# A head that sums on TensorE, later sums ahead of a mixer, and a routing with priority, in a two-block transformer kernel on one core

## The chip, the cores and the metric

The kernel runs on one core of one Trainium2 chip. The metric is the device time of an execution in microseconds; less is better. The profile times every instruction of one execution. TensorE (PE, with its weight loads as PEld), VectorE (DVE), ScalarE (ACT) and GpSimd (POOL) compute, SyncE (SP) issues most transfers. [...]

## The reference, cut to what matters

512 tokens of width 1024 pass through two blocks in float32. The first has two attention branches and a mixture of 16 experts with two experts per token, the second a mixer and an MLP twice. The parts that the change touches are these:

```python
# first_block: the head
c_act = silu(c)
mod = c_act @ ada_w + ada_b          # six vectors: shift1, scale1, gate1, shift2, scale2, gate2
h = rmsnorm(x, norm1_g) * (1 + scale1) + shift1
proj = h @ w_in
...
# hierarchical_moe: a softmax over 4 groups, the best group, its best two of 4 experts
y = hierarchical_moe(rmsnorm(x, norm2_g) * (1 + scale2) + shift2, ...)
...
# second_block, end of layer 0 and start of layer 1
x = x + rms_norm(sq_relu_mlp(h, w1, w2), norm_mlp_post[0])
h = rms_norm(x, norm_mix_pre[1])
m = mixer_c(h, ...)
```

## The kernel before, in words

Activations stand transposed, features on the 128 partitions in 8 chunks (k) and tokens along the free axis. A float32 product is made of three products of rounded parts: every operand is split into a high part (a cast on ScalarE) and a low part (a subtraction on VectorE), and `mm3` (L196, L199, L200) issues high by high, high by low and low by high. Weights come as slabs of 128 x 1024 through a ring of raw buffers, loaded by SP (L188, L1130) and split by `split` (L168 on ScalarE, L169 on VectorE).

**The head** is `first_products`. It lies under a manual schedule: on each of the five engines the instructions run in the order of the code. x comes in four transfers, then the first quarter of the modulation's weights (`fetch(0)`, L609), then slabs. ScalarE squares x chunk by chunk (L644, L647), VectorE adds the squares up (L648), four products with a column of ones sum over the partitions (`col_sum`, L326), GpSimd takes the power -0.5 (L344), and four products spread the result over the partitions (L353). The first modulation is made in quarters q of 256 shift and 256 scale columns: `ada` multiplies eight raw chunks by their entry of c and adds them on VectorE (L617, L619, L620), `columns` sums over the partitions with four single-column products (L628) and turns the sums into factors on ScalarE (L631, L632), and `modulate` makes two chunks of h (L636 and L638 on ScalarE, L639 on VectorE). x was multiplied by the norm before (L654, seven of eight chunks on GpSimd). The products of five slabs (two queries, two keys, and the forget gate as number 2) accumulate in five banks; quarter q of h gives each slab two chunks, six products. `NAT` is the slab behind which the next quarter's `columns` and `modulate` stand, `NPE` how many of the eight terms go to TensorE as raw chunks. A float32 product with one column shows as two records.

**The routing.** `route_half` makes the logits of half the tokens (L1072, two transposes L1075, the copy L1076) and the rows of the normed tokens (additions L1082 on GpSimd and VectorE, transposes L1085, copies L1086). `route` is some hundred small VectorE instructions (from L1372); in it `early` makes the one-hot rows (L1220) and gathers the first expert's tokens by products with the token rows (L1225). Two weight slabs are split ahead of the expert loop, held behind the last instruction `last_hi` of the norm on ScalarE. Outside the manual schedule a scheduler orders every engine by priority, which is the order of the code unless `first(n)` raises it by n places. After the routing a branch on the number of overflowing tokens stands on all engines, then the experts' loop.

**The sums for the second mixer.** `halves` makes the last product of an MLP in two halves of the tokens; `post` does the norm and the residual of a half chunk by chunk, as a side line that advances one step with each step of the main line (`weave`). At the end of it the squares' sums for the next norm go to TensorE (`col_mean`, four products L326), `mix_left` takes the power on GpSimd (L1552) and spreads it (L1557). `LATE[save][hb]` is the number of steps that half hb lets pass before these sums; `LATE[1]` is for the first MLP, ahead of `mixer_c`, where the second half's side line advances half a step per step of the main line.

## Time and profile before

| | us |
|---|---|
| median of 3 runs | 2283.05 |
| lowest and highest run | 2279.7 and 2284.46 |
| the profiled execution, its own time | 2282.78 |
| its span from the first to the last instruction | 2281.1 |
| TensorE busy | 2167.1 (95%) |
| VectorE busy | 1393.0 (61%) |
| ScalarE busy | 1109.9 (49%) |
| GpSimd busy | 422.6 (19%) |

The page gives busy times, the span in 40 slices with the granted clock, and the costliest groups. A timeline row has start, length, engine, line, operation, tiles written <- read, shapes and count; in brackets stand the idle time of the engine before it and what ended that. A window row gives busy time and count of each engine in a stretch, and the granted clock.

### The profile page before, as it was taken

How to read it: one execution, taken by the hardware profiler on the slowest of the kernel's cores; microseconds unless marked ns; L12 is line 12 of the kernel's file. 1: busy time of each engine (PE TensorE's matmuls, PEld its weight loads, DVE VectorE, ACT ScalarE, POOL GpSimd, SP SyncE). 2: the span in 40 equal slices, each digit the busy share in tenths (PEclk: the TensorE clock that was granted, in tenths of full speed). 3: DMA queues.
4: the chain of work that ended last, by engine and by line, in shares of the span. 5: the costliest groups of instructions: out<-in, count | busy, mean ns of one | idle time of the engine just before them, and what ended most of it. 6: DMA issues, size and time to landing. Idle time of an engine off the chain costs nothing. (4 is left out here: it accounts for less than half of the span.)

```text
span 2281.1 us, 31923 instructions
## 1 busy us (share of the span) xinstructions
PE 2167.1 (95%) x12164; PEld 1809.7 (79%) x12164; DVE 1393.0 (61%) x2002; ACT 1109.9 (49%) x1856; POOL 422.6 (19%) x468
## 2 busy tenths in 40 slices
PE   5999999979999999899999999999999999999996
PEld 4778778967888788678998888997666689888886
DVE  8577775568999964666543344565767846344343
ACT  3545542348888854445553233443655647332231
POOL 4111000231111142110400000350324433000004
PEclk9999999989999989999999999999999999999998
DMA  6464265569999741224332222342122142332321
GB/s 242 140 185 118 88 204 164 184 223 345 353 358 355 270 154 45 69 78 151 100 111 97 98 94 100 110 135 55 49 71 54 43 158 89 117 101 93 101 74 38
DMA packets 127154, 320.08 MB, mean 140 GB/s; under 512 B 24751, under 2 KB 30127, under 8 KB 126994
## 3 DMA queue, kind: packets, MB, share of 16 engines
q1 hardware_dynamic: 111934, 286.56, 36.8%
q0 software_dynamic: 11200, 22.91, 4.2%
q10 hardware_dynamic: 3860, 8.51, 1.0%
q8 instruction: 97, 1.59, 0.3%
q14 instruction: 63, 0.52, 0.1%
HBM read 296.31 MB, written 18.69 MB: 138 GB/s over the span
## 5 line engine op out<-in xcount | busy, mean ns | idle before, releaser
L196 PE MATMUL acc<-h_hi,w_hi 128*128 128x512 f32 (+1 forms) x1464 | 515.7, 352 | 3.5 <-DVE q L429 1.5
L200 PE MATMUL acc<-h_hi,w_lo 128*128 128x512 f32 (+1 forms) x1464 | 509.1, 348 | 1.2 <-DVE w_lo L169 1.2
L199 PE MATMUL acc<-h_lo,w_hi 128*128 128x512 f32 (+1 forms) x1464 | 508.7, 348 | 0.0
L169 DVE TENSOR_TENSOR w_lo<-x_raw,w_hi 128x1024 fp32r<-128x1024 f32 x260 | 317.8, 1231 | 189.8 <-ACT w_hi L168 185.2
L168 ACT CAST w_hi<-x_raw 128x1024 fp32r<-128x1024 f32 x260 | 271.0, 1046 | 283.8 <-PE acc L199 246.6
L196 PEld LDWEIGHTS acc<-h_hi,w_hi 128*128 128x128 f32 x1464 | 279.5, 191 | 36.9 <-issue 2.7
L200 PEld LDWEIGHTS acc<-h_hi,w_lo 128*128 128x128 f32 x1464 | 278.9, 190 | 35.9 <-DVE w_lo L169 2.5
L199 PEld LDWEIGHTS acc<-h_lo,w_hi 128*128 128x128 f32 x1464 | 279.0, 191 | 29.7 <-issue 0.7
L169 DVE TENSOR_TENSOR w_lo<-w_raw,w_hi 128x1024 fp32r<-128x1024 f32 (+2 forms) x141 | 166.8, 1184 | 145.0 <-ACT w_hi L168 141.3
L168 ACT CAST w_hi<-w_raw 128x1024 fp32r<-128x1024 f32 (+2 forms) x141 | 143.6, 1019 | 222.1 <-PE acc L199 199.3
L196 PE MATMUL acc<-act_hi,w_hi 128*128 128x512 f32 (+1 forms) x640 | 223.0, 349 | 0.0
L199 PE MATMUL acc<-act_lo,w_hi 128*128 128x512 f32 (+1 forms) x640 | 222.6, 348 | 0.0
L200 PE MATMUL acc<-act_hi,w_lo 128*128 128x512 f32 (+1 forms) x640 | 222.4, 348 | 0.0
L283 POOL TENSOR_TENSOR acc<-acc,sq 128x256 f32<-128x256 f32 x60 | 55.5, 926 | 721.0 <-ACT sq L282 720.2
L196 PEld LDWEIGHTS acc<-act_hi,w_hi 128*128 128x128 f32 x640 | 121.9, 190 | 15.3 <-ACT act_hi L1621 0.3
L199 PEld LDWEIGHTS acc<-act_lo,w_hi 128*128 128x128 f32 x640 | 121.9, 190 | 15.0
L200 PEld LDWEIGHTS acc<-act_hi,w_lo 128*128 128x128 f32 x640 | 121.8, 190 | 15.0
L506 DVE TENSOR_TENSOR pl<-pexp,ph 128x512 fp32r<-128x512 f32 x144 | 113.9, 803 | 25.9 <-ACT ph L505 25.1
L1626 DVE TENSOR_TENSOR m<-m,acc 128x512 f32<-128x512 f32 (+1 forms) x64 | 35.2, 552 | 138.7 <-PE acc L200 138.7
L470 DVE TENSOR_REDUCE mx<-acc 128x1 f32<-128x128 f32 x192 | 89.2, 484 | 37.9 <-PE acc L469 36.3
L504 ACT ACTIVATE pexp<-sT 128x512 f32<-128x512 f32 x144 | 82.5, 573 | 32.2 <-PE sT L495 14.2
L196 PE MATMUL gu<-w_hi,xh 128*128 128x512 f32 x240 | 95.5, 398 | 0.0
(593 smaller groups left out, 4422.0 us busy)
## 6 DMA issues: line engine op xcount, KB each, us to landing
x_raw<-mlp_w SPq DMA_DIRECT2D x90, 512.0 KB
w_raw<-mlp_w SPq DMA_DIRECT2D x48, 512.0 KB
x_raw<-w_down SPq DMA_DIRECT2D x40, 512.0 KB
x_raw<-w_up SPq DMA_DIRECT2D x39, 512.0 KB
x_raw<-w_gate SPq DMA_DIRECT2D x38, 512.0 KB
w_raw<-w_in SPq DMA_DIRECT2D x20, 512.0 KB
h_raw<-w_up SPq DMA_DIRECT2D x19, 512.0 KB
h_raw<-w_gate SPq DMA_DIRECT2D x18, 512.0 KB
```

Source lines behind the costliest of these rows:

```text
L168: nc.scalar.copy(hi[:, :n], raw[:, :n])
L169: (eng or nc.vector).tensor_sub(lo[:, :n], raw[:, :n], hi[:, :n])
L196: mm(ps, l[0], r[0], start=start, stop=False)
L199: mm(ps, l[0], r[1], start=False, stop=False)
L200: return mm(ps, l[1], r[0], start=False, stop=stop).ins
L283: (eng or nc.gpsimd).tensor_add(acc[:, a:a + 256], acc[:, a:a + 256], sq)
L470: self.last_max = nc.vector.reduce_max(mx[:, c0 + qb:c0 + qb + 1], ps[:, :n], axis=AX.X).ins
L504: nc.scalar.activation(e[:, :o], ps[:, :o], AF.Exp)
L506: nc.vector.tensor_sub(pt[1][:, :o], e[:, :o], pt[0][:, :o])
L1626: nc.vector.tensor_add(self.m[:, i, tok], self.m[:, i, tok], ps)
```

## The change

In the head the squares are no longer added on VectorE: each chunk's square goes to TensorE as four products with a column of ones. The first quarter's eight raw chunks go to TensorE as well, four ahead of the spread of the norm and four behind it; of the later quarters three of eight (`NPE = 3`). The multiplication by the norm joins that by the scale on VectorE (`scale`), and the head's first slabs are split behind the first modulation. The third and fourth slab are loaded ahead of the second quarter. `NAT` becomes one value per quarter. `LATE[1]` goes from (34, 10) to (44, 14). In the routing the logits' two VectorE instructions and all of `route` get a priority 4000 places higher, and the two slabs split ahead wait for the last one-hot row on VectorE instead of the norm on ScalarE.

```diff
@@ -50,8 +50,8 @@
 RATE = 1.0
 APB = 2
 EV = 1000
-NPE = 0
-NAT = 1
+NPE = 3
+NAT = (3, 2, 2)
 GY = 2
 VK = 1
 PK = 1
@@ -59,7 +59,7 @@
 R1 = 0.4
 R5 = 0.4
 APP = 0
-LATE = ((40, 22), (34, 10))
+LATE = ((40, 22), (44, 14))
 
 
 
@@ -610,7 +610,7 @@
                 return [out[k // 2][:, k % 2 * 512:k % 2 * 512 + 512] for k in range(NC)]
 
             def ada(raws):
-                acc = [sp.tile([P, 512], F32, name="ada_sum", bufs=4) for i in range(2)]
+                acc = [sp.tile([P, S], F32, name="ada_sum", bufs=4) for i in range(2)]
                 for k in range(NC - NPE):
                     ck, a = self.c_act[:, k:k + 1], acc[k % 2]
                     if k < 2:
@@ -620,39 +620,49 @@
                 nc.vector.tensor_add(acc[0], acc[0], acc[1])
                 return acc[:1]
 
-            def columns(q, raws, acc):
-                src = [(raws[k], self.c_act[:, k:k + 1]) for k in range(NC - NPE, NC)]
-                for l, r in src + [(a, self.ones[:, :1]) for a in acc]:
+            def columns(q, raws, ks, acc=()):
+                for l, r in [(raws[k], self.c_act[:, k:k + 1]) for k in ks] + [(a, self.ones[:, :1]) for a in acc]:
                     for c in range(4):
                         d = 8 * (c // 2) + 2 * q + c % 2
                         nc.tensor.matmul(pa[:, d:d + 1], l[:, c * P:(c + 1) * P], r, start=False, stop=True,
                                          skip_group_check=True)
+
+            def mods(q):
                 for k in (2 * q, 2 * q + 1):
                     nc.scalar.mul(self.mod[:, 8 + k:9 + k], pa[:, 8 + k:9 + k], self.v("norm1_g", k))
                 nc.scalar.copy(self.mod[:, 2 * q:2 * q + 2], pa[:, 2 * q:2 * q + 2])
 
-            def modulate(q):
-                for k in (2 * q, 2 * q + 1):
-                    nc.scalar.mul(x[:, k], x[:, k], self.mod[:, 8 + k:9 + k])
-                    b = self.mod[:, k:k + 1]
-                    nc.scalar.activation(self.h[0][:, k], x[:, k], AF.Identity, bias=b)
-                    nc.vector.scalar_tensor_tensor(self.h[1][:, k], x[:, k], b, self.h[0][:, k], op0=OP.add,
-                                                   op1=OP.subtract)
+            def scale(k):
+                nc.vector.scalar_tensor_tensor(x[:, k], x[:, k], self.mod[:, 8 + k:9 + k], r, op0=OP.mult, op1=OP.mult)
+
+            def parts(k):
+                b = self.mod[:, k:k + 1]
+                nc.scalar.activation(self.h[0][:, k], x[:, k], AF.Identity, bias=b)
+                nc.vector.scalar_tensor_tensor(self.h[1][:, k], x[:, k], b, self.h[0][:, k], op0=OP.add,
+                                               op1=OP.subtract)
 
             raws = [fetch(0)]
-            acc = sp.tile([P, S], F32, name="acc", tag="ada_sum", bufs=4)
-            nc.scalar.square(acc, x[:, 0])
-            for k in range(1, NC):
+            cs = self.pn.tile([P, S], F32, name="csum", tag=self.ntags[0])[:, :4]
+            nc.tensor.matmul(cs, self.zb, self.zb[:, :4], start=True, stop=True)
+            for k in range(NC):
                 sq = sp.tile([P, S], F32, name="sq", bufs=2)
                 nc.scalar.square(sq, x[:, k])
-                nc.vector.tensor_add(acc, acc, sq)
+                for j in range(4):
+                    nc.tensor.matmul(cs[:, j:j + 1], sq[:, j * P:(j + 1) * P], self.ones[:, :1], start=False, stop=True,
+                                     skip_group_check=True)
             c = sp.tile([P, 4], F32, name="rs_c")
-            nc.scalar.activation(c, self.col_sum([acc]), AF.Identity, bias=self.eps, scale=1.0 / D)
-            r = self.spread(self.rsqrt(c), sp)
-            sums = [ada(raws[0])]
-            for k in range(NC):
-                (nc.gpsimd if k else nc.vector).tensor_mul(x[:, k], x[:, k], r)
-            slabs = [self.slab(w[i], NC) for i in range(2)]
+            nc.scalar.activation(c, cs, AF.Identity, bias=self.eps, scale=1.0 / D)
+            c = self.rsqrt(c)
+            columns(0, raws[0], range(4))
+            r = self.spread(c, sp)
+            columns(0, raws[0], range(4, NC))
+            mods(0)
+            scale(0)
+            scale(1)
+            parts(0)
+            slabs = [self.slab(w[0], NC)]
+            parts(1)
+            slabs.append(self.slab(w[1], NC))
             raw = sp.tile([P, NC * 16], F32, name="fa_raw")
             nc.sync.dma_start(raw, self.t["w_fa"])
             fa = tuple(sp.tile([P, NC, 16], F32R, name=n) for n in ("fa_h", "fa_l"))
@@ -660,11 +670,9 @@
             nc.scalar.copy(fa[0], rv)
             nc.vector.tensor_sub(fa[1], rv, fa[0])
             slabs.append(fa)
+            slabs += [self.slab(w[i], NC) for i in (2, 3)]
             raws.append(fetch(1))
-            columns(0, raws[0], sums[0])
-            modulate(0)
-            sums.append(ada(raws[1]))
-            slabs += [self.slab(w[i], NC) for i in (2, 3)]
+            sums = ada(raws[1])
             ps = [pp.tile([P, S], F32, name="pst") for _ in range(3)] + [self.ptile() for _ in range(2)]
 
             def mm(n, q):
@@ -673,16 +681,19 @@
                     self.mm3(ps[n][:hi.shape[-1]], (hi[:, k], lo[:, k]), (self.h[0][:, k], self.h[1][:, k]), k == 0,
                              k == NC - 1)
 
-            for q in range(4):
+            for q in range(3):
                 if q < 2:
                     raws.append(fetch(q + 2))
-                    sums.append(ada(raws[q + 2]))
                 for n in range(5):
-                    if q < 3:
-                        mm(n, q)
-                        if n == NAT:
-                            columns(q + 1, raws[q + 1], sums[q + 1])
-                            modulate(q + 1)
+                    mm(n, q)
+                    if n == NAT[q]:
+                        columns(q + 1, raws[q + 1], range(NC - NPE, NC), sums)
+                        mods(q + 1)
+                        for k in (2 * q + 2, 2 * q + 3):
+                            scale(k)
+                            parts(k)
+                        if q < 2:
+                            sums = ada(raws[q + 2])
             mm(2, 3)
             fg = self.forget(ps[2], tmp, sp.tile([16, S], F32R, name="nf_h", tag="sq", bufs=2), nf)
             next(fg)
@@ -1069,11 +1080,13 @@
             self.mm3(ps[:20, :256], (self.rw[0][:, k], self.rw[1][:, k]), (h[0][:, k], h[1][:, k]),
                      k == 0, k == NC - 1)
         lt = self.rp.tile([P, 256], F32, name="rf", bufs=2)
-        nc.vector.tensor_scalar(lt[:20], ps[:20, :256], self.rb, None, op0=OP.add)
+        with self.first(4000):
+            nc.vector.tensor_scalar(lt[:20], ps[:20, :256], self.rb, None, op0=OP.add)
         ps = self.ptile()
         for b in range(2):
             nc.tensor.transpose(ps[:, 20 * b:20 * b + 20], lt[:20, b * P:(b + 1) * P], self.idf[:20, :20])
-        nc.vector.tensor_copy(self.L[:, 2 * hb:2 * hb + 2], ps[:, :40].rearrange("p (b c) -> p b c", b=2))
+        with self.first(4000):
+            nc.vector.tensor_copy(self.L[:, 2 * hb:2 * hb + 2], ps[:, :40].rearrange("p (b c) -> p b c", b=2))
         yield 1
         for k in range(0, NC, 2):
             ps = self.ptile()
@@ -1217,8 +1230,8 @@
                 nc.vector.tensor_add(m, E[:, 0, :, 0], E[:, 1, :, 0])
                 oh = mp.tile([P, NC, P], F32R, name="oh", tag="xl").bitcast(F32)
                 for b in range(4):
-                    nc.vector.tensor_scalar(oh[:, b], self.slot, pos[:, b, 0:1], m[:, b:b + 1], op0=OP.is_equal,
-                                            op1=OP.mult)
+                    self.last_oh = nc.vector.tensor_scalar(oh[:, b], self.slot, pos[:, b, 0:1], m[:, b:b + 1],
+                                                           op0=OP.is_equal, op1=OP.mult).ins
                 ps = [self.ptile().rearrange("p (k t) -> p k t", k=4) for _ in range(2)]
                 for k in range(NC):
                     for b in range(4):
@@ -1226,7 +1239,8 @@
                                          start=(b == 0), stop=(b == 3))
                 return ps
 
-            idx, sw, nov, ovx, ftok, ps = self.route(rp, mp, pt, early)
+            with self.first(4000):
+                idx, sw, nov, ovx, ftok, ps = self.route(rp, mp, pt, early)
             for q in range(2):
                 c = slice(4 * q, 4 * q + 4)
                 nc.scalar.copy(x[0][:, c], ps[q])
@@ -1235,7 +1249,7 @@
             my = self.pool(es, "moe_y")
             gather(1, xgs[1])
             self.parts = deque(self.pairs(self.wp, 2) + self.pairs(xw, 1))
-            with tc.issue_after(self.last_hi):
+            with tc.issue_after(self.last_oh):
                 split = [parts(*ahead.popleft()) for _ in range(2)]
             hl, self.parts = self.parts, deque(self.pairs(xw, 1))
             n = nc.values_load(nov[0:1, 0:1], min_val=0, max_val=7)
```

## Rows read from the trace of the kernel before

**Rows 1.** The page, parts 1 and 5.
```profile
PE 2167.1 (95%) x12164; PEld 1809.7 (79%) x12164; DVE 1393.0 (61%) x2002; ACT 1109.9 (49%) x1856; POOL 422.6 (19%) x468
...
L168 ACT CAST w_hi<-x_raw 128x1024 fp32r<-128x1024 f32 x260 | 271.0, 1046 | 283.8 <-PE acc L199 246.6
```

**Rows 2.** Windows: PE, PEld, DVE, ACT, POOL busy (count); clock; DMA.
```profile
38.00:43.00 5.00, 5.00 (x16) 3.35 (x17) 5.00 (x8) 3.07 (x7) 0.00 (x0) 0.50 0.93 317
826.00:834.80 8.80, 8.73 (x41) 8.73 (x42) 5.01 (x11) 5.09 (x15) 3.17 (x5) 0.50 0.29 95
1477.20:1483.60 6.40, 6.01 (x26) 5.74 (x27) 2.04 (x5) 1.94 (x6) 4.65 (x5) 0.50 0.91 297
1511.20:1517.90 6.70, 6.70 (x33) 6.62 (x33) 4.59 (x9) 2.45 (x7) 3.97 (x10) 0.50 0.90 269
```

**Rows 3.** Timeline of the head: start, length, engine, line, tiles, count.
```profile
5.80 0.63 ACT L644 ACTIVATE acc<-x 128x512 f32<-128x512 f32 x1 [2.77 <-DMA x<-x]
...
19.76 1.81 PE L628 MATMUL acc<-ones,ada_sum 128*128 128x1 f32 x8
...
20.67 12.26 POOL L654 TENSOR_TENSOR x<-x,rstd 128x512 f32<-128x512 f32 x7 [2.83 <-ACT rstd L356]
21.57 4.17 DVE L169 TENSOR_TENSOR w_lo<-x_raw,w_hi 128x1024 fp32r<-128x1024 f32 x2 [0.26 <-ACT w_hi L168]
...
28.74 0.79 PE L199 MATMUL pst<-h_lo,w_hi 128*128 128x512 f32 x1 [3.47 <-DVE h_lo L639]
...
33.35 0.40 PE L200 MATMUL pst<-h_hi,w_lo 128*128 128x512 f32 x1
```

**Rows 4.** Timeline of the head's last rounds, 48.8 to 70 us.
```profile
49.05 0.95 PE L628 MATMUL acc<-ones,ada_sum 128*128 128x1 f32 x8
...
49.86 0.40 PE L196 MATMUL pst<-h_hi,fa_h 128*16 128x512 f32 x1
...
58.92 0.72 ACT L638 ACTIVATE h_hi<-x,mod 128x512 fp32r<-128x512 f32 x1
...
59.68 0.75 DVE L639 SCALAR_TENSOR_TENSOR h_lo<-x,mod,h_hi 128x512 fp32r<-128x512 f32 x1 [5.64 <-ACT h_hi L638]
...
65.79 1.23 DVE L169 TENSOR_TENSOR w_lo<-w_raw,w_hi 128x1024 fp32r<-128x1024 f32 x1 [1.64 <-ACT w_hi L168]
...
68.50 0.39 PE L200 MATMUL acc<-h_hi,w_lo 128*128 128x512 f32 x1
```

**Rows 5.** Timeline of the routing, 485 to 510 us.
```profile
485.68 2.34 DVE L169 TENSOR_TENSOR w_lo<-w_raw,w_hi 128x1024 fp32r<-128x1024 f32 x2
...
485.81 0.30 PE L1075 MATMUL acc<-idf,rf 20*128 20x20 f32 x2 [0.42 <-DVE rf L1072]
...
486.24 2.45 POOL L1082 TENSOR_TENSOR rf<-h_half 128x256 f32<-128x256 f32 x1 [5.19 <-PE acc L1075]
...
487.95 0.18 DVE L1076 COPY L<-acc 128x40 f32<-128x40 f32 x1
488.06 0.91 DVE L1082 TENSOR_TENSOR rf<-h_half 128x256 f32<-128x256 f32 x1
...
493.67 0.58 ACT L1086 COPY rows<-acc 128x512 f32<-128x512 f32 x1 [0.85 <-PE acc L1085]
...
496.29 9.49 PE L1225 MATMUL acc<-oh,rows 128*128 128x128 f32 x64 [0.59 <-DVE oh L1220]
...
509.87 0.47 PE L196 MATMUL gu<-w_hi,x_raw 128*128 128x512 f32 x1 [3.60 <-PEq L1244]
```

**Rows 6.** Timeline of TensorE, 1474 to 1510 us.
```profile
1477.23 0.56 PE L326 MATMUL csum<-ones,acc 128*128 128x1 f32 x2 [3.08 <-DVE acc L283]
...
1481.99 1.23 PE L1557 MATMUL spread<-idf,mix_rcol 128*128 128x128 f32 x4 [0.36 <-POOL mix_rcol L1552]
...
1509.38 0.35 PE L326 MATMUL csum<-ones,acc 128*128 128x1 f32 x2 [2.07 <-DVE acc L283]
```

**Rows 7.** Timeline of TensorE, 818 to 840 us.
```profile
826.07 2.72 PE L1320 MATMUL gu<-gg,sq 128*128 128x2 f32 x12 [0.84 <-ACT sq L1318]
```

## The prediction

> **What bounds the kernel now.** I read the page's busy times first: TensorE is busy for 95% of the span [rows 1]. [...] Then the table of windows, for the granted clock of single stretches [rows 2]; the timeline of the head [rows 3, 4]; the timeline of the routing [rows 5]; and TensorE's timeline where the second block's first MLP hands over to the second mixer [rows 6], with one row of the same engine for the clock [rows 7]. In all of them the reader should look at what the next product of TensorE waits for.
>
> In the head the 120 products of the first five slabs are held up until 28.74 us, because the low parts are late (VectorE's two splits took 4.17 us beside seven multiplications on GpSimd, 12.26 us); 12 are done by 33.75 and all by 68.9 [rows 3, 4]. From 49.86 to 68.50 there are 78 products and one group of four single-column products of 0.81 us (49.05 to 49.86): (18.87 - 0.81) / 78 = 0.23 us a product [rows 4]. The window of 38 to 43 us was at half clock [rows 2], and a single-column product (two records) took 1.81 us for four early in the head, so 0.43 us each without the tail, against 0.20 us at full clock [rows 3, 4].
>
> **Part 1, the head.** It moves three sums from VectorE to TensorE as products with one column. Removed: the adding up of the squares and the eight-term sums of the first modulation on VectorE, three of eight terms in the three later ones, the multiplication of x by the norm on GpSimd and one ScalarE pass per chunk. Added: 32 - 4 products for the squares, 32 - 4 for the first modulation's columns, 12 more for each of three later ones. The order in this block is the order in the code on every engine, so it can be walked.
>
> The first square ends at 6.43 [rows 3]. 32 products at 0.43 are 13.8 us, the 32 of the first modulation as much again, and the spread of the norm between them, four products too, some 1.8: 35.8 us. A square takes ScalarE 0.63 us [rows 3] against 1.7 for its four products, so TensorE sets the pace. Only then do the modulation's factors go out: 0.3, the scaling on VectorE 0.75 (the same form and size as the low part), the high part on ScalarE 0.72 [rows 4], then the first slab's cast of 1.05 [rows 1], which now stands behind them: first product at 38.7. On VectorE follow a split (1.23), a low part (0.75) and a split (1.23) [rows 4]: the second slab's products are free at 41.9, and 12 are done at about 44, which was 33.75 before. What else the diff touches in this block (names, the loop's bounds) issues nothing. That is 10.3 us later; the cost of GpSimd beside VectorE is gone and is counted in it.
>
> The other 108 products: 108 x 0.23 = 24.8 us; three groups of 16 single-column products at 0.20 = 9.7 us. After each group the next round needs factors, scaling, high and low part twice in turn: 0.3 + 2 x (0.75 + 0.72 + 0.75) and some handing over, 5.0 us, and 0.46 us of products behind it. The first time only one slab (1.38) and the round's own first slab (1.38) lie beside that, a wait of 2.7; the two other times two slabs do, a wait of 1.3 each: 5.3 us. Before, three slabs stood there, and rounds two and three did not wait. Half clock behind the start and behind the longest waits: 3 us (between 0 and 6). The sum is 44 + 42.8 = 86.8 against 68.9: **+17.5 us** (+15 to +21). Loads: the slabs' weights go ahead of the second modulation's on SP, whose buffers are free at 27 and 36 us, far ahead of their use; the third and fourth come free with the splits. If that cover is gone, a load of 512 KB costs some 1.7 us at the 317 GB/s of 38 to 43 us [rows 2]. TensorE has no other work that could hide the head, so I count it in full.
>
> Everything hangs on the clock in the two runs of single-column products. The nearest rows: from 826.07 TensorE runs two-column products back to back (12 records in 2.72 us), and from 826 to 834.8 it is busy for 8.73 of 8.80 us, with wider products towards the end; the clock reads 0.50 throughout [rows 2, 7]. So I take the lower level. [...]
>
> **Part 2, the routing.** Now the copy of the logits waits for two splits of prefetched weights on VectorE (485.68, 2.34 us) and ends up at 487.95, and a token row's addition of 0.91 follows before the first routing step [rows 5]. Its transposes end at 486.1 [rows 5]. Ahead of both it wins 1.75 + 0.9 us, and something from GpSimd, whose token row took 2.45 us beside the splits. The token rows, due before the products at 496.29, were in place at 494.25 [rows 5]; they start earlier too, as the splits are gone. I take **-3 us**, down to -4.5. The MoE's first product at 509.87 follows from this chain [rows 5]. The splits come behind the one-hot rows and have until the first product for it; the reload of their two buffers on SP comes later by as much, for products that are some slabs away. In the other direction: the splits were tied to a ScalarE instruction and are now tied to a VectorE one, so the two casts of 1 us may go ahead of the norm's activations there, and up to +2 us is possible.
>
> **Part 3, the later sums.** TensorE waits 3.08 us for the squares at 1477.23, 0.36 at 1481.99, 2.07 at 1509.38 [rows 6], and both times half clock follows: 6.01 us busy at 0.50, then 6.70 [rows 2]; half of each is lost. Together 5.5 + 3.0 + 3.35 = 11.9 us. Ten steps later in the first half puts 30 products of half the width ahead of the sums, some 3.5 us; four steps later in the second half are eight steps of the main work with six such products each, some 5.5 us. Both are more than the wait. What is late next: the spread, which needs the power on GpSimd. From the end of the sums (1477.23 + 1.7) it took until 1481.99, 3 us [rows 6], and now two steps, 0.7 us, stand between. New waits of 2.4 us in all, so **-9.5 us** (-5 to -11.9). The second half's weights are split by then and VectorE has pauses, so nothing else need be late.
>
> **The sum.** +17.5 - 3 - 9.5 = +5 us. The profiled execution took 2282.78 us (span 2281.1), 0.3 under the median of 2283.05. I say 2288 us. Some 0.2%, 4.6 us, is about what a measurement of this kernel can tell from no change, so the forecast lies at that bound.
>
> **The rivals.**
> - *The single-column products raise the clock.* Place: the sums of squares. After some ten products at 0.43 the other 54 take 0.20 each: the factors go out at about 23 us; with some 9 to the twelfth product and 39.8 for the rest, plus 1 to 2 of half clock, the products end at about 73.4, +4.5. With the other parts -8 us: 2275. For it: the engine is busy without a pause for 29 us. Against: 826 to 834.8 [rows 2, 7]. A rise at time t saves half of what is left up to 35.8, so it decides the sign from a rise before about 26 us on. Chance 0.18.
> - *The sums for the mixer only wait elsewhere.* The spread is held for the full 3 us both times, and the clock falls as before. Then part 3 gives 4, and the sum is +10.5: 2293. For it: the power stands behind additions on GpSimd. Against: those have time while TensorE goes on. Chance 0.12.
> - *The routing does not move.* VectorE's order is made by the scheduler, and the copy may still land behind other work, or the casts go in front. Part 2 is 0 to +2, and the sum +8 to +10: 2292. Chance 0.08.
>
> **How the numbers follow.** The forecast has 0.62; its own range is 2282 to 2294 from the bounds of the parts. About half of it lies over the bound of 4.6 us and half within. The first rival is nearly all faster, the others slower. Faster 0.19, same 0.35, slower 0.46. The range reaches from the middle of the first rival to above the second: 2275 to 2297.
>
> **What would show it.** In the changed profile: the first product of the slabs near 39 us and the last near 87; single-column products 0.43 us apart up to 36 us; no wait over 1 us before the two sums at the mixer and a clock of 1.00 behind them; the logits' copy directly behind its transpose, and the MoE's first product 20.8 us after the end of that transpose instead of 23.8. The head's last product below 75 us, or a new wait before the mixer's spread, would make the prediction wrong.

## The result, and the profile after

| | before | after |
|---|---|---|
| median (6 runs each) | 2283.64 us | 2308.95 us |
| lowest and highest | 2279.7 and 2285.77 | 2302.15 and 2316.11 |
| ratio, 95% interval | | 1.011 [1.0091, 1.0128] |
| span of the profiled execution | 2281.1 us | 2306.2 us |

The change makes the kernel slower by 1.1%. The forecast was 2288 us with a range to 2297: the direction was right, the size lies outside.

The page of the kernel after, its head and part 1, where [rows 1] stand for before:

```profile
span 2306.2 us, 32250 instructions
PE 2206.1 (96%) x12349; PEld 1847.3 (80%) x12349; DVE 1375.7 (60%) x1984; ACT 1105.9 (48%) x1848; POOL 409.2 (18%) x461
```

VectorE, ScalarE and GpSimd lost a little work, and TensorE, which bounds the kernel, got 39 us more. Where in time the 25.1 us came can be read by following the same instruction through both timelines:

| instruction | before | after | later by |
|---|---|---|---|
| the head's last product of 512 columns | 68.50 | 88.56 | 20.06 |
| the transposes of the logits | 485.81 | 508.05 | 22.24 |
| the experts' first product | 509.87 | 532.45 | 22.58 |
| the norm's spread (L353) ahead of the second mixer | 1459.18 | 1480.08 | 20.90 |
| the first product of scores (L468) behind that mixer | 1580.07 | 1604.03 | 23.96 |
| the end | 2281.1 | 2306.2 | 25.1 |

So in this pair of profiles the head costs 20 us, the routing's stage neither gives nor takes, and the mixer's stage, which should have given 9.5 us, takes 3.1. The other shifts, of 1.1 to 2.2 us and not all of one sign, lie in stages that the change does not touch.

**The head.** TensorE's timeline after, against [rows 3, 4] (start, length, engine, line, tiles, count; in brackets the idle time before and what ended it):

```profile
6.33 13.81 PE L651 MATMUL csum<-ones,sq 128*128 128x1 f32 x64 [2.37 <-ACT sq L649]
20.00 6.96 PE L627 MATMUL acc<-c_act,w_raw 128*128 128x1 f32 x32
26.83 2.06 PE L353 MATMUL spread<-idf,rs_r 128*128 128x128 f32 x8
28.68 6.83 PE L627 MATMUL acc<-c_act,x_raw 128*128 128x1 f32 x32
38.39 0.79 PE L196 MATMUL pst<-h_hi,w_hi 128*128 128x512 f32 x1 [2.89 <-ACT w_hi L168]
...
46.76 2.73 PE L627 MATMUL acc<-c_act,x_raw 128*128 128x1 f32 x24
49.36 1.03 PE L627 MATMUL acc<-ones,ada_sum 128*128 128x1 f32 x8
...
54.54 0.50 PE L196 MATMUL pst<-h_hi,w_hi 128*128 128x512 f32 x1 [0.26 <-ACT h_hi L640]
55.33 0.50 PE L199 MATMUL pst<-h_lo,w_hi 128*128 128x512 f32 x1 [0.29 <-DVE h_lo L641]
...
58.68 3.08 PE L627 MATMUL acc<-c_act,more_raw 128*128 128x1 f32 x24
61.62 1.84 PE L627 MATMUL acc<-ones,ada_sum 128*128 128x1 f32 x8
...
88.56 0.39 PE L200 MATMUL acc<-h_hi,w_lo 128*128 128x512 f32 x1
```

TensorE runs single-column products from 6.33 to 35.5 almost without a pause, 0.43 us each (64 records in 13.81). That is the spacing of such products where the clock reads 0.50 (8 records from 61.62 to 63.33); where it reads 1.00 it is half of that, 0.22 (24 records from 46.76 to 49.36). So by the spacing TensorE does not leave the lower level, 0.50, there, although the windows before 44 us print 1.00. The first slab product starts at 38.39. Behind 46.76 only two waits are left, 0.26 and 0.29 us. Yet the clock falls, as the windows show (busy time and count of PE, PEld, DVE, ACT, POOL; granted clock; DMA share; GB/s):

```profile
51.00:54.00 3.00, 3.00 (x8) 1.69 (x6) 1.89 (x3) 0.95 (x2) 0.00 (x0) 0.50 0.79 268
61.00:67.50 6.50, 6.50 (x22) 5.63 (x23) 2.17 (x3) 1.84 (x5) 0.00 (x0) 0.50 0.00 0
68.00:74.00 6.00, 6.00 (x36) 4.67 (x35) 3.83 (x7) 0.00 (x0) 0.00 (x0) 1.00 0.56 172
75.00:81.00 6.00, 6.00 (x20) 5.13 (x21) 2.16 (x3) 1.73 (x5) 0.00 (x0) 0.50 0.00 0
```

Each of the three stretches at 0.50 begins in or right behind a group of single-column products, and TensorE is busy for the whole of it.

**The routing**, where [rows 5] stand for before:

```profile
508.05 0.40 PE L1087 MATMUL acc<-idf,rf 20*128 20x20 f32 x2 [0.42 <-DVE rf L1084]
508.48 0.20 DVE L1089 COPY L<-acc 128x40 f32<-128x40 f32 x1 [0.16 <-PE acc L1087]
508.72 0.17 DVE L1386 TENSOR_REDUCE gm<-L 128x4 f32<-128x16 f32 x1
...
512.39 0.42 DVE L1095 TENSOR_TENSOR rf<-h_half 128x256 f32<-128x256 f32 x1 [0.96 <-PE acc L1098]
...
517.49 1.11 DVE L1233 TENSOR_SCALAR oh<-slot,bp,first 128x128 f32<-128x128 bf16 x4
...
524.22 1.22 DVE L169 TENSOR_TENSOR w_lo<-w_raw,w_hi 128x1024 fp32r<-128x1024 f32 x1
...
532.45 0.77 PE L196 MATMUL gu<-w_hi,x_raw 128*128 128x512 f32 x1 [4.18 <-PEq L1258]
```

The first step and the one-hot rows of the kernel before:

```profile
488.90 0.15 DVE L1372 TENSOR_REDUCE gm<-L 128x4 f32<-128x16 f32 x1
...
495.89 1.12 DVE L1220 TENSOR_SCALAR oh<-slot,bp,first 128x128 f32<-128x128 bf16 x4
```

The copy is directly behind its transposes, 0.43 us after their start instead of 2.14, and the first step (L1386, L1372 before) comes 0.67 us after that start instead of 3.09. But three row additions still stand between the routing's steps on VectorE and wait there for the rows' transposes, 2.2 us in all (0.96 is the longest): the one-hot rows come 9.44 us after the transposes' start, 10.08 before. The two splits, put off, now stand among the steps behind them (1.22 us each, at 520.73 and 524.22), and the experts' first product comes 24.40 us after the transposes against 24.06.

**The second mixer.** What TensorE waited for, first before (1470 to 1580 us), then after (1490 to 1560): total us, times, longest.

```profile
PE csum L326 <- DVE acc L283: 5.1, 2, 3.1
```

```profile
PE spread L1571 <- POOL mix_rcol L1566: 6.4, 2, 5.9
PE acc L199 <- DVE w_lo L169: 2.3, 1, 2.3
```

The waits ahead of the sums are gone, and in their place stands a longer one ahead of the spread. The timeline after shows why:

```profile
1498.63 1.81 POOL L283 TENSOR_TENSOR acc<-acc,sq 128x256 f32<-128x256 f32 x1 [1.66 <-ACT sq L282]
...
1500.10 0.15 DVE L337 TENSOR_SCALAR rs_c<-csum 128x2 f32<-128x2 f32 x1
...
1503.46 0.72 POOL L283 TENSOR_TENSOR acc<-acc,sq 128x256 f32<-128x256 f32 x1 [0.53 <-ACT sq L282]
1504.22 0.42 ACT L282 ACTIVATE sq<-m 128x256 f32<-128x256 f32 x1 [0.83 <-POOL acc L283]
1504.71 0.72 POOL L283 TENSOR_TENSOR acc<-acc,sq 128x256 f32<-128x256 f32 x1 [0.53 <-ACT sq L282]
1505.39 0.71 POOL L1566 TENSOR_TENSOR mix_rcol<-rs_c,mh 128x2 f32<-128x2 f32 x1
1506.16 1.22 PE L1571 MATMUL spread<-idf,mix_rcol 128*128 128x128 f32 x4 [5.90 <-POOL mix_rcol L1566]
```

The argument of the power is ready at 1500.25, but on GpSimd the power stands behind five additions of the second half's squares and runs at 1505.39. The last four come 1.25 us apart, with square and addition in strict turn. The clock falls with this wait, for longer than [rows 2] show (14 us where they have 6.4 and 6.7), and once more behind the second wait:

```profile
1501.00:1515.00 14.00, 8.84 (x40) 8.58 (x41) 1.47 (x4) 2.74 (x7) 5.70 (x9) 0.51 0.21 79
1535.60:1538.80 3.20, 3.20 (x17) 3.20 (x17) 1.33 (x4) 0.47 (x1) 0.00 (x0) 0.50 0.99 289
```

### The profile page after: what moved, and what is told of

Its sections match the earlier page's. It is cut to its first block, busy times and chain, and to the rows that moved or that the text cites. A ratio compares the mean times of both kernels' runs of the same rounds, so it can differ in the third digit from the quotient of the medians.

```text
span 2306.2 us, 32250 instructions
## 1 busy us (share of the span) xinstructions
PE 2206.1 (96%) x12349; PEld 1847.3 (80%) x12349; DVE 1375.7 (60%) x1984; ACT 1105.9 (48%) x1848; POOL 409.2 (18%) x461
## 5 line engine op out<-in xcount | busy, mean ns | idle before, releaser
L169 DVE TENSOR_TENSOR w_lo<-x_raw,w_hi 128x1024 fp32r<-128x1024 f32 (+1 forms) x258 | 314.0, 1225 | 189.8 <-ACT w_hi L168 183.5
L168 ACT CAST w_hi<-x_raw 128x1024 fp32r<-128x1024 f32 (+1 forms) x258 | 269.2, 1046 | 284.0 <-PE acc L199 246.7
```

Source lines behind the costliest of these rows:

```text
L168: nc.scalar.copy(hi[:, :n], raw[:, :n])
L169: (eng or nc.vector).tensor_sub(lo[:, :n], raw[:, :n], hi[:, :n])
```

## The experiments

**One part alone.** e1_head takes the head alone (`NPE`, `NAT`, `first_products`), e2_late the line of `LATE` alone, e4_route the hunks of the routing alone, e9_no_head both of these without the head.

```diff
-LATE = ((40, 22), (34, 10))
+LATE = ((40, 22), (44, 14))
```

> The head of the change alone; routing and sums as before. Theory A (each part has its own loss): the last product of the head starts at 88.6 us as in the changed kernel, 20.1 us later than before, and the stages behind it keep their lengths within 1 us: 2303 to 2306 us, +20 to +22. Rival B (the later start is what spoils the routing and the second mixer): +25 as with the whole change, about 2308 us. Rival C (the prediction's own term): +17.5, 2301 us.

> The later sums of the second mixer alone. Theory A: TensorE no longer waits at the first column sum but reaches the first spread with five square additions still ahead of the power on POOL, so it waits about 5.9 us there and about 2.3 us at a weight split behind it: +2 to +4, 2286 to 2288 us. Rival B (the prediction's term): -9.5, 2274 us, with no wait over 1 us ahead of the spreads. Rival C (a loss only in company of the new head): -3, 2280 us.

> The routing part alone. Theory A: the copy of the logits stands directly behind its transpose (0.4 us after its start instead of 2.1), but the additions of the token rows that stand between the routing steps on VectorE wait for their buffers and the splits fall between the routing and the token gather, so the first product of the experts starts 24.0 to 24.4 us after the transpose as before (24.06): 2282.5 to 2284.5 us. Rival B (the prediction's term): 21 us after the transpose and -3 us, 2280.5 us.

> The changed kernel with the old head: routing and later sums together. Theory A (the head alone makes the kernel slower, and the two other parts give nothing): 2283 to 2288 us, within 0.2% of the kernel before. Rival B (what the whole change costs beyond the head's 20 us comes from the two other parts in company): 2288 to 2291 us. Rival C (the prediction's terms, -3 and -9.5): 2273 us.

| | median us (runs) | before, same chip | ratio, interval |
|---|---|---|---|
| e1_head | 2302.13 (4) | 2284.8 | 1.0077 [1.006, 1.0094] |
| e2_late | 2287.48 (10) | 2284.8 | 1.0008 [0.9994, 1.0022] |
| e4_route | 2285.01 (10) | 2284.8 | 1.0 [0.999, 1.0009] |
| e9_no_head | 2283.07 (12) | 2284.07 | 0.9996 [0.9982, 1.0011] |

The head alone makes the kernel slower, by some 17.6 us; in its profile the last product is at 88.54, 20.04 us later than before. The sums alone show the wait of 5.9 ahead of the spread and 2.3 for the low part, the routing alone its copy at +0.33 and its first product at +24.01 us from the transposes: the time of neither can be told from before. The parts add up to 1.0085, the whole to 1.011; their intervals touch, and whether the 6 us or so between them are more than scatter stays open.

One profile says little of the mixer's stage, from the norm's spread to the first product of scores. Nine profiles with the old sums there (before, e1, e4, e7, e8, e10, e11, e14, e15) have 118.2 to 122.7 us for it, and the three with the later sums 119.2 (e2, e9) and 124.0 (after).

**What holds the spread.** e3_late_adds puts the second half's square additions on VectorE; e5_late_held gives the last square of the first half, which the late sum reads, a buffer of its own, so that the two buffers of the second half's squares are free; e6_held does that with the old sums.

```diff
-            self.sq_half(accs[hb], self.m[:, i, tok], seen[hb])
+            self.sq_half(accs[hb], self.m[:, i, tok], seen[hb], self.nc.vector if save and hb else None)
```

```diff
-                self.sq_half(acc, x[:, k, tok], k, nc.vector if k >= PSQ else nc.gpsimd)
+                if hold is not None and k == NC - 1:
+                    acc.append(hold.tile([P, 256], F32, name="held"))
+                    nc.scalar.square(acc[1], x[:, k, tok])
+                else:
+                    self.sq_half(acc, x[:, k, tok], k, nc.vector if k >= PSQ else nc.gpsimd)
```

> As the run with the later sums alone, and the second mixer's square additions of the second half of the tokens go to VectorE, so that no addition stands ahead of the power on POOL. Theory A (the power waits in POOL's queue): the wait at the first spread falls from about 5.9 to under 2.5 us, and the time is 3 to 7 us under that of the later sums alone, 2280 to 2284 us. Rival B (VectorE is what the chain waits for, and gets more to do): the wait goes elsewhere and the time is that of the later sums alone or more, 2286 us or above.

> As the run with the later sums alone, but the last square of the first half, which the late column sum reads, lies in a buffer of its own instead of in one of the two that the squares share. Theory A (the late sum keeps one of the two square buffers, so every square of the second half waits for the addition before it on POOL): the squares on ScalarE and the additions on POOL run two deep, the additions follow each other at 0.72 to 0.95 us instead of 1.25 us, and the wait at the first spread falls from 5.9 to 2.5 to 4.5 us. Rival B (the additions wait for the products and VectorE's sums of m): the wait stays within 0.5 us of 5.9.

> The kernel before with that buffer alone, sums at their old place. Theory A: the wait at the first column sum stays at 3.08 us (it waits for the first half's last addition, which the buffer does not touch) and the second half's squares end up to 2 us earlier: 0 to -2 us. Rival B: no change in any wait.

Measured: e3 2282.59 (10 runs), 0.9991 [0.9977, 1.0004], the spread waits 3.9 us; e5 2285.14 (8), 1.0003 [0.9979, 1.0028]; e6 2286.49 (8), 1.0006 [0.9985, 1.0027], with the waits ahead of the sums unchanged (5.1 in 2). The timelines, e3 first, then e5:

```profile
1480.35 0.15 DVE L337 TENSOR_SCALAR rs_c<-csum 128x2 f32<-128x2 f32 x1
...
1481.60 1.22 PE L1557 MATMUL spread<-idf,mix_rcol 128*128 128x128 f32 x4 [3.90 <-POOL mix_rcol L1552]
```

```profile
1478.53 4.00 POOL L283 TENSOR_TENSOR acc<-acc,sq 128x256 f32<-128x256 f32 x4 [0.34 <-ACT sq L282]
...
1482.48 0.71 POOL L1556 TENSOR_TENSOR mix_rcol<-rs_c,mh 128x2 f32<-128x2 f32 x1
1483.25 1.22 PE L1561 MATMUL spread<-idf,mix_rcol 128*128 128x128 f32 x4 [3.38 <-POOL mix_rcol L1556]
```

With the buffer the additions run 1.0 us apart instead of 1.25 and the wait falls from 5.89 (e2) to 3.38: the held buffer is 2.5 us of it. Most of the rest is the four additions that still end only where the power starts, as the timeline reads. In e3 the power does not queue on GpSimd any more, but the instruction that makes its argument now stands behind the additions on VectorE, 3.8 us after the sums: the queue only moved, and the wait is 3.9 where under 2.5 was expected. None of the three times can be told from that of before.

**What could be had at the mixer.** e12_next_stage has e6's buffer, `LATE[1] = (42, 10)`, and the spread five steps later, with the rest of the first side line running on into the mixer.

```diff
-        for _ in range(2):
+        for _ in range(7):
...
-        weave((RATE for _ in out[1]), tails[0])
-        return tails[1]
+        for _ in out[1]:
+            next(tails[0], None)
+        return chain(*tails)
```

> The kernel before with the second mixer's sums two steps ahead of the changed place, the square in a buffer of its own, and the spread put off into the next stage's first products, so that TensorE has work while the power waits on POOL. Theory A (the waits are of the chain of squares, additions and power; TensorE waits wherever the order makes it meet the chain, and only work put in between hides it): no wait over 1 us at the first column sum, 0.5 to 2 us at the spread (5.9 with the later sums, 3.4 with the buffer), waits of the second half at 2 us as before; the stage 2 to 5 us shorter than before: 2278 to 2283 us. Rival B (the first half's chain does not bound the stage; what is saved there is waited for at the second half's sum): that wait grows from 2.07 us by as much as the first ones shrink, and the time is within 1 us of before.

Measured: 2277.97 (10 runs), 0.9972 [0.9953, 0.9992]. The longest waits from 1460 to 1560 and two windows:

```profile
PE acc L199 <- DVE w_lo L169: 1.4, 1, 1.4
PE spread L1561 <- POOL mix_rcol L1556: 0.8, 1, 0.8
```

```profile
1484.00:1498.00 14.00, 13.03 (x108) 12.62 (x107) 11.51 (x20) 8.07 (x18) 6.38 (x7) 1.00 0.32 109
1498.00:1520.00 22.00, 19.85 (x162) 19.25 (x162) 17.33 (x27) 12.48 (x26) 16.51 (x28) 1.00 0.67 181
```

The clock stays at 1.00 up to 1550, and the stage, from the norm's spread to the first product of scores, is 10.0 us shorter than before: more than expected. Before, then here, over the whole stage:

```profile
1459.20:1580.10 120.90, 113.86 (x754) 104.30 (x754) 72.09 (x129) 54.37 (x104) 48.26 (x72) 0.92 0.35 103
1457.70:1568.60 110.90, 106.70 (x754) 98.04 (x754) 73.39 (x129) 54.48 (x104) 50.22 (x72) 0.98 0.38 112
```

TensorE stands idle for 4.2 us instead of 7.0, the second half's wait of 2.07 [rows 6] among what went, and the same 754 records take 106.70 us instead of 113.86: most of the gain is the clock. So about 10 of the 9.5 to 11.9 us that the prediction counted were there in the profile (in the timed runs some 6.4, between 1.8 and 10.7); putting the sums off, without putting off what depends on them, does not fetch them. e12 moves the sums, the spread and the side lines and has the buffer, all at once; beyond e2, e5 and e6 no run shows which of these is needed.

**The row additions.** e10_rows_pool is e4_route with all row additions on GpSimd.

```diff
-                (nc.vector if hb and i else nc.gpsimd).tensor_add(f, h[0][:, k + i].bitcast(F32), h[1][:, k + i].bitcast(F32))
+                nc.gpsimd.tensor_add(f, h[0][:, k + i].bitcast(F32), h[1][:, k + i].bitcast(F32))
```

> The routing part alone, with the four token-row additions of the second half that stood between the routing steps on VectorE put on POOL. Theory A (VectorE waits at those additions for their buffers, which costs the routing chain 1.07 us): the one-hot starts 8.2 to 8.6 us after the start of the logits' transpose instead of 9.4 (10.1 before), the one-hot products as much earlier. Rival B (the chain of small operations itself sets the time): 9.2 us or more. In both the first product of the experts comes at 22.5 to 24 us, since the splits and the token steps lie behind the one-hot products.

Measured: 2281.35 (8 runs), 0.9993 [0.9975, 1.0011]. The one-hot rows come 7.71 us after the transposes, 9.36 in e4 and 8.2 to 8.6 expected, and the first product 22.62 instead of 24.01: the additions on VectorE had kept back that gain of 1.4 to 1.7 us. Against the run-to-run spread it is too small to be told.

**What the head's 20 us are.** e7_ada_vector is e1_head with five of the first quarter's eight terms on VectorE, e14_few_columns with one raw term instead of three in the later quarters (`NPE = 1`), e15_squares_vector with the squares added on VectorE; e8_warm puts ten products of 128 columns, whose result is not used, ahead of the sums.

```diff
-            columns(0, raws[0], range(4))
+            sums = ada(raws[0], N0)
+            columns(0, raws[0], range(NC - N0, NC))
             r = self.spread(c, sp)
-            columns(0, raws[0], range(4, NC))
+            columns(0, raws[0], (), sums)
```

```diff
+            for _ in range(10):
+                nc.tensor.matmul(ww, self.idf, self.idf, start=True, stop=True)
```

> The head alone, and of its first quarter five of the eight modulation blocks are summed on VectorE instead of all eight on TensorE (squares still summed on TensorE). Theory A (the single-column products at the lower clock level, one after another on TensorE, are what makes the head late): 64 of these records go and 32 come in their place, at 0.216 us each 6.9 us; the first product starts at 31 to 32.5 us instead of 38.4 and the head's last product 6 to 7.5 us earlier, at 81 to 83 us; +13 to +15 to the kernel before. Rival B (the transfers of the modulation blocks set the start): the first product starts within 2 us of 38.4 us.

> The head alone as in the change, but in its three later quarters one block of eight instead of three is summed on TensorE by single-column products, the other seven on VectorE. Theory A (each later group of 32 records costs its own time and a stretch at the lower clock behind it): the first product stays at 38.4 us, the granted clock has at most one lower stretch between 45 and 85 us instead of three, and the last product starts at 78 to 82 us instead of 88.5. Rival B (VectorE cannot follow with seven blocks, which is why the change moved them): the last product at 87 us or later.

> The head alone as in the change, but the squares are added on VectorE as before, with 8 records of column sums on TensorE instead of 64. Theory A (the 64 records at 0.216 us are on the path, but the modulation blocks land only at 11 to 15 us, so not all of their 13.8 us comes back): the first product at 33 to 35.5 us instead of 38.4, the last product 3 to 5.5 us earlier than 88.5. Rival B (the modulation columns alone fill TensorE until 38 us): less than 1 us earlier.

> The head alone, with ten products of 128 columns whose result is not used put in front of the sums of squares on TensorE, while it waits for x. Theory A (single-column products do not bring the clock to its upper level, and what is done before x lands does not last): the records of the sums still come 0.43 us per pair, and the head's last product moves by less than 1 us. Rival B (the clock is low only because TensorE had been idle): the records come at about half that distance behind the ten products, the first product starts 8 to 14 us earlier than 38.4 us, and the time falls by as much.

| | median us (runs) | ratio, interval | first product | last product, against e1 |
|---|---|---|---|---|
| e1_head | 2302.13 (4) | 1.0077 [1.006, 1.0094] | 38.45 | 88.54 |
| e7_ada_vector | 2295.46 (6) | 1.0054 [1.0031, 1.0077] | 31.64 | 78.26, -10.3 |
| e14_few_columns | 2299.37 (5) | 1.0076 [1.0054, 1.0099] | 38.39 | 83.29, -5.3 |
| e15_squares_vector | 2300.8 (3) | 1.0073 [1.0046, 1.0099] | 34.34 | 82.97, -5.6 |
| e8_warm | 2311.88 (3) | 1.0101 [1.0048, 1.0153] | 40.35 | 88.93, +0.4 |

In these profiles the three sums moved to TensorE cost about 10, 5 and 6 us, together a little more than the 20; in the timed runs the intervals of e7, e14 and e15 overlap with that of e1. Not all of it is the columns' own time. The stretches at 0.50 behind the later groups are 6.7, 3.4 and 6.7 us long in e1. In e7, whose later groups are the same, they are 3.6 and 3.4, with none behind the second group: 9.8 us less at 0.50, so that by estimate half of them, some 5 us of what e7 gives back, are the clock's. e14 has two as well, the first of them 5 us behind its group and after four waits of 0.29 to 0.68, and came in above the 78 to 82 expected (windows, first behind the second group of e7, then the two stretches of e14):

```profile
55.40:63.60 8.20, 7.34 (x30) 4.88 (x30) 6.23 (x10) 1.91 (x5) 0.00 (x0) 1.00 0.17 52
...
55.20:58.50 3.30, 3.30 (x10) 2.16 (x9) 3.30 (x6) 0.00 (x0) 0.00 (x0) 0.50 0.01 2
72.30:75.50 3.20, 3.20 (x9) 2.52 (x9) 2.01 (x3) 1.18 (x4) 0.00 (x0) 0.50 0.01 3
```

In e8 the wider products ahead do not help (timeline): the sums take the same 13.8 us. But the ten products themselves stand 0.22 us a record apart, like the norm's spread at 28.8 us (8 records in 1.85) and not like that at 1483.7 (4 records in 0.47), so they ran at the lower level too. What the sums would do behind a stretch at the upper level no run shows.

```profile
3.83 4.62 PE L648 MATMUL acc<-idf 128*128 128x128 f32 x20
8.31 13.79 PE L654 MATMUL csum<-ones,sq 128*128 128x1 f32 x64
```

**The rest of the head without its sums, and all three.** e11_head_vector is the kernel before with the scaling of the change's head, but squares and the first quarter's terms on VectorE, one raw term later on (`NPE = 1`, `NAT = (1, 1, 1)`), the two first slabs split ahead of the modulation, and two terms of each next sum ahead of the scaling. e13_all_three joins e11's head, e10's routing and e12's mixer.

> The old head's sums (squares and the first quarter's modulation sums on VectorE, one block of eight on TensorE in the later quarters) with the new head's scaling (x times modulation times norm in one operation on VectorE, none on POOL). Theory A (the column products on TensorE made the head late, the scaling did not; before, POOL's 12.26 us of scaling slowed VectorE's splits and differences): the first three-product group is done by 27 us instead of 29.8, the first modulation columns come at 33 to 36 us instead of 38, and the head's last product at 64 to 69 us (68.5 before, 88.6 with the change): -4 to 0 us. Rival B (the scaling on VectorE is part of the loss): last product at 72 us or later, +4 us or more.

> The three repaired parts together: the head with its sums on VectorE and the scaling in one operation, the routing with the token-row additions on POOL, and the second mixer's spread in the next stage. Theory A (the parts stand in stages far from each other and add up): the head's last product 3.2 us earlier than before, the one-hot 1.8 to 2.4 us earlier behind its transpose, the second mixer's stage 8 to 10 us shorter: 2268 to 2274 us. Rival B (what is gained in one part is lost in a later wait): 2276 us or more.

e11: 2281.9 (10 runs), 0.9994 [0.9976, 1.0011], last product at 65.34, 3.2 us earlier than before (68.46 to 69.37 in the nine profiles with the old head). Its timeline, against 21.57 and 28.74 in [rows 3]:

```profile
21.57 2.36 DVE L169 TENSOR_TENSOR w_lo<-x_raw,w_hi 128x1024 fp32r<-128x1024 f32 x2 [1.91 <-ACT w_hi L168]
...
25.46 0.80 PE L196 MATMUL pst<-h_hi,w_hi 128*128 128x512 f32 x1 [3.88 <-ACT h_hi L642]
```

With the multiplications gone from GpSimd the two splits take 2.36 us instead of 4.17. So the new head without its sums is a gain of 3.2 us in the profile, too small for the timed runs to tell, and the sums on TensorE bury it; how much of it is the scaling alone is not separated from e11's new order. e13: 2272.46 (6 runs) beside 2285.49, 0.9942 [0.9921, 0.9963]: a version that beats both kernels. Its head ends at 65.53 and its mixer's stage is about 10 us shorter; a stretch at the lower clock from 1775 to 1795, where before has one of 7 us (1791 to 1798, 0.52), gave some 7 us back in the profiled execution, without a longer wait there.

## Why the prediction was right in direction and wrong in size

**Part 1, +17.5 forecast, +20.06 measured in the profile and some +17.6 (between 13.7 and 21.5) in e1's timed runs.** The sum was miscounted by 0.4: 86.8 against 68.9 is +17.9. The walk to the twelfth product was right: 38.7 and 44 forecast, 38.39 and 44.0 measured, and with it the choice of the lower level for the single-column products. The remaining 108 products took 44.6 us against 42.8, by two errors that nearly cancel. The waits of 5.3 us behind the column groups are 0.55. And "Half clock behind the start and behind the longest waits: 3 us (between 0 and 6)" is the term that failed: the three column groups take 12.8 us instead of 9.7 (46.76 to 50.25, 58.68 to 63.33, 72.31 to 76.93), and some 30 products behind them run 0.43 apart instead of 0.23, another 6.5 us. That is 9.6 us in place of 3, and not behind waits: TensorE was busy throughout. The prediction's own row, where busy two-column products stood at 0.50 [rows 2, 7], bore on these groups as much as on the first ones, and was not applied to them. Why the clock falls behind such groups while TensorE is busy stays open. That the two errors cancel is luck.

The rival built on a rise of the clock did not happen: 29 us of single-column products, with only the norm's spread among them, did not raise it (0.43 us a product from 6.33 to 35.5). The rise after "some ten products at 0.43" that it reckons with did not come: the 64 records of the squares' sums took 13.81 us after and 13.79 in e8.

**Part 2, -3 forecast, +0.3 measured, and nothing that e4's timed runs can tell.** The step that failed is "The MoE's first product at 509.87 follows from this chain": what was won ahead of the first step did not reach it. The 1.75 + 0.9 us came nearly as forecast: the first step is 2.4 us earlier, 1.7 of it the copy. But the other row additions were left among the steps and now waited 2.2 us there, so that 0.6 us was left at the one-hot rows, and the splits, which had been ahead, took that and more back before the first product. e10 shows what the additions held: 1.4 us.

**Part 3, -9.5 forecast, +3.1 measured in the profile, -1.6 in e2's and e9's, and some +1.8 (between -1.4 and +5.0) in e2's timed runs.** The step that failed is "New waits of 2.4 us in all": they are 5.9 and 2.3. The 3 us from sums to spread were taken from the kernel before as a fixed length, but later in time the power meets five additions of the next half on GpSimd. This is the rival "the sums for the mixer only wait elsewhere", which had 0.12, named that very queue, and put "those have time while TensorE goes on" against it. It allowed 3 us each; the buffer that the late sum holds made the first 2.5 us more (e5). The prediction had named a new wait before the spread as what would make it wrong.

In all, of the 20.1 us by which the profiled pair exceeds the forecast, 2.6 come from part 1, 3.3 from part 2 and 12.6 from part 3; the rest, 1.6, lies in stages that the change does not touch. By the timed runs of the parts the head came as forecast, 3 us are missing from the routing and 11 from the sums, and some 6 us of the whole belong to no part.

The range was too narrow by its own terms as well: the bounds of the parts, +21, +2 and -5, add up to +18 or 2301 us, not to the 2294 that it states. The measured 2308.95 lies above that too.

## What to carry to other kernels

When a small result is made later on purpose, follow it through the queue it will meet at the new time, and ask which buffer its late reader now holds; moving only the producer moved the wait here (5.9 us ahead of the spread in e2, 3.9 in e3). Sums over partitions by single-column products look free on a busy TensorE, but here those at the start ran at the lower clock (0.43 us each), and behind 14 of the 15 later groups of 32 records the wide products ran at 0.50; VectorE had the time for them (the head's last product at 65.34 in e11 and 65.53 in e13, 88.56 after). Compare waits, not only stage lengths: the same waits gave stages that differ by 4.7 us through the clock (e2 and after).

## What the runs showed of the hardware that had not been expected

- TensorE was busy for whole stretches and was granted 0.50 of its clock in them: 3.00 of 3.00 us at 51, 6.50 of 6.50 at 61, 6.00 of 6.00 at 75, each behind a group of 32 single-column records. Such a stretch followed 14 of the 15 groups of 32 records (after, e1, e7, e8, e15), 4 of the 9 groups of 16 (e14, e11, e13, some with waits of up to 1.15 us in or behind the group) and neither of the groups of 8 at 49 and 57 us before. The size of the group alone did not set it: e7 with 32 records and e14 with 16 had the same two stretches, of 3.2 to 3.6 us.
- The same code and waits did not give the same clock. With the old waits the stretch at the lower level behind the first one was some 7 us before [rows 2] and 10.2 in e1 (1498.8 to 1509, 0.50). With the new ones it was 14 us both in e2 and after, but the products behind the mixer's two-column products ran at 1.00 in e2 (1551 to 1556) and at 0.64 after (1571.5 to 1578.3; 0.71 before), and behind the second wait the clock read 1.00 in e2 (1516 to 1522) and 0.50 after (1535.6 to 1538.8). With nearly the same idle time (8.8 and 8.9 us) TensorE was busy for 110.5 us of the stage in e2 and 115.0 after, so the stage came out 1.6 us shorter than before in e2 and 3.1 longer after.
- Two splits on VectorE took 4.17 us beside GpSimd's multiplications and 2.36 without them (e11), and the two low parts behind them (L639 before, L643 in e11) 3.43 and 1.42.
- The table of windows gives a clock of 1.00 for the kernel after from 0 to 44 us, while its products of 512 columns stood 0.43 us apart up to there (40.24 to 43.66), which is the spacing from 63.90 to 67.31, where the clock reads 0.50. At 1.00 they stood 0.23 apart (83.00 to 88.56). So the start of the head is read here by the spacing.
